# Splitting every third weight unit on GpSimd instead of VectorE: a two-layer hybrid decoder on one core

## The chip, the cores and the metric

The kernel runs on one core of a Trainium2 chip. The core has a matrix engine (TensorE, PE in the profile), three engines for elementwise work (VectorE or DVE, ScalarE or ACT, GpSimd or POOL), a queue that mostly issues DMAs (SyncE or SP), and 16 DMA engines. Every engine works through its own instructions in order, and waits on semaphores for the others. The metric is the device time of one execution in microseconds. The kernel before takes 1306.37 us, the median of three runs (1305.67 to 1306.95).

## What is computed

A trunk of two layers over 256 positions of width 2048, all in float32. Each layer adds a mixer's output to its scaled input and normalises the rows.

```python
for layer in range(DEPTH):                      # DEPTH = 2
    if layer % 2 == 0:
        h = ssd_moba_mixer(x, in0_w[i], ..., out0_w[i])
    else:
        h = s5_mixer(x, in1_w[i], ..., glu_w[i], out1_w[i])
    x = layer_norm(DEEPNORM_ALPHA * x + h, ln_g[layer], ln_b[layer])
```

The even layer projects x by one wide matrix (`in0_w`) to xs, z, B, C, dt and to queries, keys, values and a gate. xs, B and C pass a causal convolution and feed a state-space scan, whose result is gated by silu(z); the queries, keys and values feed attention; both results are mapped back by `out0_w`. The odd layer projects by `in1_w` to u and a gate, runs a diagonal complex scan, and then has three matrix products in a row: `y @ glu_w`, whose two halves make `ga * sigmoid(gb)` (the gated products), and, after a silu gate, `@ out1_w` (the last product).

## The kernel before

**Products in three parts.** TensorE is given its operands in the type fp32r. So that nearly all bits of float32 count, each operand is cut in two: a high part, the value copied to fp32r, and a low part, raw minus high. A product is then the sum of three: activations' high by weights' high, high by low, and low by high.

**Weight units.** The weights are read from memory in 462 units of 128 x 1024 elements (512 KB). They are numbered in the order in which TensorE uses them:

| units | what |
|---|---|
| 0 to 15 | B and C |
| 16 to 47 | xs |
| 48 to 79 | z |
| 80 to 207 | queries, keys, values, gates |
| 208 to 283 | out0 |
| 284 to 347 | in1 |
| 348 to 363 | first two blocks of the gated products |
| 364 to 429 | the other blocks of the gated products (66 units, `STREAM`) |
| 430 to 461 | out1, the last product |

**Making a unit ready.** `split_to(i)` traces, for each unit up to i, a load into a buffer `raw` (SyncE's queue, L361), the high part `wh` by ScalarE (L367), and the low part `wl` by VectorE (L372). For units 2 to 461 that is one instruction each, on 128 x 1024 elements. `raw`, `wh` and `wl` have four buffers each (`bufs=4`); each product calls `split_to(unit[0] + 3)`, so a unit is made ready about three units ahead of its use, and ScalarE can write `wh` of unit n only when TensorE is done with unit n - 4.

**Using a unit.** For xs and z (`product_wide`), a unit takes eight pairs of matmuls, one with `wh` (L478) and one with `wl` (L479). In the other products here a unit takes 12 matmuls (`xmm`, L422), a third of them with `wl`. In `STREAM` (`product_fast`), some steps work on sums of weight blocks and cover one half of the positions only: such a unit takes 6 matmuls (L521), two of them with `wl`, and is used up in half the time.

**Sums of weight blocks.** In the stream, the operand `raw` of a step is often a `block` that other blocks have been added to. Some of these sums are made by VectorE (L326), others by DMAs that add while they store. The adding DMAs are issued from GpSimd's queue (L324), each behind the split that still has to read the block, and in a fixed order among themselves.

**Order of the work.** The order of each engine's instructions is made when the program is built, by a scheduler that runs a model of the times; `tc.issue_after(ins)` keeps what is traced under it behind `ins` in the queue of `ins`'s engine, and is no wait for another engine. Elementwise work of the layers (`jobs`, `back`) is traced between the units by `run`, each piece behind the split instructions of the unit two ahead (`splits`).

**GpSimd's other work.** It computes part of softplus for dt (`soft2`, `soft3`, L734 to L745) while xs is being multiplied, adds up squares (L1092) in and after z, makes tables of phases (L906 to L909) and a rotary addition (L1143) during attention, and issues a part of the DMAs. It has no split.

The gated products are one stream of steps for three groups of two column blocks:

```python
HEAD = "p1 p1 n2 n2 p3 n2 p3 q5 q5 v2 v2 n2 q7 q7 p2 n1 n1 | p4 p4 p2 n1 n1".split()
FLOW = "q5 q5 p3 n2 p3 n2 v2 v2 n2 n2 q7 q7 p2 n1 n1 | p4 p4 p2 n1 n1".split()
```

Steps n1 and n2 are whole units, the others the half ones; "|" stands for the two p1 of the next group.

Of the kernel before, what the change touches and what calls it, by code (L numbers as in the profile page):

```python
# [9 lines left out]
F32 = mybir.dt.float32  # L10
F32R = mybir.dt.float32r
AF = mybir.ActivationFunctionType
OP = mybir.AluOpType
# [8 lines left out]
CU = KT // UK  # L22
# [15 lines left out]
def _stream():  # L38
    out, seen = [], {}
    for g in range(GROUPS):  # L40
        for s in FLOW if g else HEAD:
            names = [(g, s)] if s != "|" else [(g + 1, "p1")] * 2 * (g + 1 < GROUPS)
            for name in names:
                seen[name] = seen.get(name, -1) + 1
                out.append(name + (seen[name],))
    return out


STREAM = _stream()
# [140 lines left out]
def trunk(tc, io, out):  # L190
    nc = tc.nc
    V, A, G, T = nc.vector, nc.scalar, nc.gpsimd, nc.tensor
    count = [0]

    def nm(s):
        count[0] += 1
        return f"{s}_{count[0]}"

    with ExitStack() as top:
# [26 lines left out]
        units = []  # L226
# [7 lines left out]
        def hook(table, g, k, key, off, *what):  # L234
            table.setdefault(place[g, key, 0] + off, []).append((g, k, sources[g]) + what)
# [26 lines left out]
        chain = [len(units) + CU]  # L262
        units += [io["wglu"][i] for i in range(2 * CU)]
        start = len(units)
        place.update({key: start + i for i, key in enumerate(STREAM)})
        for g in range(GROUPS):
            n1, n2 = ([io["wglu"][CU * (2 + 2 * g + c) + u] for u in range(CU)] for c in range(2))
# [8 lines left out]
        for g in range(GROUPS):  # L276
            for k in range(2):
# [11 lines left out]
                hook(then, g, k, "p1", k, "add", "a", "b")  # L289
                hook(then, g, k, "v2", k, "add", "a", "d")  # L290
        units += [io["wo1"][i] for i in range(io["wo1"].shape[0])]
        ready = {}
        nsplit = [0]
        early = {}
        loaded = []
        conv = []
        splits = {}
# [7 lines left out]
        def prepare(*what):  # L305
            with ExitStack() as pin:
                if what[0] == 0:
                    pin.enter_context(tc.issue_after(tail["y"].ins))
                prepared(*what)
# [18 lines left out]
        def split_to(i):  # L328
            while nsplit[0] <= min(i, len(units) - 1):
                n = nsplit[0]  # L330
                for what in first.get(n, ()):
                    prepare(*what)
                if n in early:
                    with tc.issue_after(loaded[-1].ins):
                        early.pop(n)()
                if n in held_raw:
                    raw = blocks[held_raw[n]]
                elif n in room:
                    raw = keep[0].tile([P, UK, 512], F32R, tag=room[n], name=nm("raw")).bitcast(F32)
                else:  # L340
                    raw = st.tile([P, UK, 512], F32, tag="raw", name=nm("raw"))
                if n < 2:
                    wh = st.tile([P, UK, 512], F32R, tag="wh", name=nm("wh"))
                    wl = st.tile([P, UK, 512], F32R, tag="wl", name=nm("wl"))
                    for k in range(UK):
                        if k == 0:
                            xpart(n)
                        for lo, hi in ((0, 256), (256, 512)) if n + k == 0 else ((0, 512),):
                            loaded.append(nc.sync.dma_start(raw[:, k, lo:hi], units[n][:, k * 512 + lo : k * 512 + hi]))
                            with tc.issue_after(conv[-2].ins):  # L350
                                conv.append(A.activation(wh[:, k, lo:hi], raw[:, k, lo:hi], AF.Copy))
                            with tc.issue_after(conv[-2].ins):
                                conv.append(V.tensor_tensor(wl[:, k, lo:hi], raw[:, k, lo:hi], wh[:, k, lo:hi].bitcast(F32), op=OP.subtract))
                    ready[n] = (wh, wl)
                    nsplit[0] += 1
                    continue
                if n not in held_raw:
                    with ExitStack() as pin:
                        if n >= chain[0]:
                            pin.enter_context(tc.issue_after(loaded[-1].ins))  # L360
                        loaded.append(nc.sync.dma_start(raw.rearrange("p k n -> p (k n)"), units[n]))  # L361
                pool, th, tl = (keep[0], f"wh{n % 8}", f"wl{n % 8}") if n in keep[1] else (st, "wh", "wl")
                wh = pool.tile([P, UK, 512], F32R, tag=th, name=nm("wh"))
                with ExitStack() as pin:
                    if hold[1] is not None:
                        pin.enter_context(tc.issue_after(hold[1]))
                    high = A.activation(wh, raw, AF.Copy)  # L367
                wl = pool.tile([P, UK, 512], F32R, tag=tl, name=nm("wl"))
                with ExitStack() as pin:
                    if hold[0] is not None:  # L370
                        pin.enter_context(tc.issue_after(hold[0]))
                    splits[n] = (loaded[-1], high, V.tensor_tensor(wl, raw, wh.bitcast(F32), op=OP.subtract))  # L372
                ready[n] = (wh, wl)
                for what in then.get(n, ()):
                    prepare(*what)
                nsplit[0] += 1
# [72 lines left out]
        def product(kind, hl, nu=CU, prelude=None, first=WHOLE, due=None):  # L449
            ps = banks()  # L450
            for u in range(nu):
                if prelude:
                    prelude(u)
                split_to(unit[0] + 3)
                wpair = ready.pop(unit[0])
                if kind == "w":
                    wmm(ps, u, nu, hl, wpair, first if u == 0 else WHOLE)
                else:
                    last = u == nu - 1
                    steps = [(j, o) for o in range(2) for j in range(UK)] if last else [(j, o) for j in range(UK) for o in range(2)]  # L460
                    for j, o in steps:
                        xmm(ps, o, wpair, j, hl(u * UK + j), u == 0 and j == 0, last and j == UK - 1)
                unit[0] += 1
                pump((due - 1 if due and u < due - 1 else nu - 1) - u)
            return ps
# [186 lines left out]
        with ExitStack() as l0:  # L652
# [28 lines left out]
            def xpart(k):  # L681
                xr = a4([P, S])
                (nc.sync if k else nc.scalar).dma_start(xr, io["xt"][:, k, :])
                with ExitStack() as pin:
                    if k:
                        pin.enter_context(tc.issue_after(conv[-2].ins))
                    conv.append(A.activation(xh[:, k, :], xr, AF.Copy))
                with ExitStack() as pin:
                    if k:
                        pin.enter_context(tc.issue_after(conv[-2].ins))  # L690
                    conv.append(V.tensor_tensor(xl[:, k, :], xr, xh[:, k, :].bitcast(F32), op=OP.subtract))
# [339 lines left out]
            for j in range(4):  # L1031
                raw = sz[:, 4 * j : 4 * j + 4, :]
# [921 lines left out]
```

## Time and profile before

| | |
|---|---|
| median of three runs | 1306.37 us |
| span of the profiled execution | 1304.8 us |
| TensorE busy | 1296.0 us |
| VectorE busy | 1031.8 us |
| ScalarE busy | 738.1 us |
| GpSimd busy | 349.2 us |
| splits on VectorE (L372) | 460, mean 1.25 us |

The profile is of one execution; its times count from the first instruction. Busy times overlap, since the engines work side by side. A group's row gives, behind the count, its busy time and the mean of one instruction in nanoseconds, and then the idle time of the engine ahead of it with what ended it. In the timeline a row gives start, duration, engine, line, operation, output<-input, and in brackets the idle time before. TensorE's matmuls are pipelined and their ends are modelled, so that one may show 0.39 us where the next starts 0.23 us after it. The page can't be read as "TensorE has nothing to spare" from its busy share alone; who it waited for is a view of its own.

### The profile page before, as it was taken

The page shows a single profiled execution, that of the slowest core. Times are in us where ns is not written, and L with a number is a line of the kernel's source. Part 1 is how long each engine was busy: PE and PEld are TensorE (multiplying, and loading weights), DVE is VectorE, ACT ScalarE, POOL GpSimd, SP SyncE. Part 2 cuts the span into 40 slices and gives each one's busy share as a digit, 9 for nine tenths or more (in the row PEclk, how much of TensorE's full clock was granted, in tenths as well). Part 3 has the DMA queues.
Part 4 walks back from the last instruction along what each step waited for, and adds up shares of the span by engine and source line. Part 5 has one row for each costly group of instructions (what it writes and reads, how often), then busy time and mean ns, then how long its engine had stood idle before and what let it go on. Part 6 is the DMA issues. An engine that isn't in the chain of part 4 may idle for free.

```text
span 1304.8 us, 21605 instructions
## 1 busy us (share of the span) xinstructions
PE 1296.0 (99%) x7939; PEld 1089.7 (84%) x7939; DVE 1031.8 (79%) x1694; ACT 738.1 (57%) x1000; POOL 349.2 (27%) x649
## 2 busy tenths in 40 slices
PE   9999999999999999999999999999999999999997
PEld 9988888878888888888888888888888888888885
DVE  6778977885788888888877777858989859988665
ACT  6566668865644554464475555354355557666441
POOL 0044000125035767876820110022232001110000
PEclk9999999999999999999999999999999999999999
DMA  8555566565557766767768978469999789888762
GB/s 316 177 179 188 180 209 198 190 204 178 182 197 244 233 224 228 239 210 245 235 207 291 302 186 291 170 219 324 317 292 327 245 311 241 217 249 230 257 212 80
DMA packets 100094, 300.90 MB, mean 231 GB/s; under 512 B 19378, under 2 KB 29570, under 8 KB 99476
## 3 DMA queue, kind: packets, MB, share of 16 engines
q1 hardware_dynamic: 74356, 239.81, 55.0%
q0 software_dynamic: 11232, 46.18, 13.5%
q10 hardware_dynamic: 14400, 13.54, 3.2%
q8 instruction: 62, 1.02, 0.3%
q14 instruction: 44, 0.36, 0.1%
HBM read 276.93 MB, written 21.00 MB: 228 GB/s over the span
## 4 chain that ended last, share of the span: by engine, by line
PE 95%; POOL 2%; DVE 1%; DMA 1%; issue 0%; ACT 0%; SPq 0%; POOLq 0%
PE main L422 51%; PE main L478 17%; PE main L479 9%; PE main L521 7%; PE main L445 3%; PE aux L626 2%; POOL c L906 1%; PE aux L1084 1%; PE enc L1593 1%; PE dec L1638 1%; PE aux L982 1%; PE aux L1170 0%; DMA wb<-c 0%; POOL c L909 0%; DMA raw<-in_wi 0%; PE dec L1634 0%
## 5 line engine op out<-in xcount | busy, mean ns | idle before, releaser
L372 DVE TENSOR_TENSOR wl<-raw,wh 128x1024 fp32r<-128x1024 f32 x400 | 497.0, 1247 | 194.6 <-ACT wh L367 191.8
L367 ACT ACTIVATE wh<-raw 128x1024 fp32r<-128x1024 f32 x400 | 421.9, 1059 | 403.1 <-PE main L422 184.0
L422 PE MATMUL main<-wh,A 128*128 128x512 f32 x1216 | 392.5, 394 | 0.0
L478 PE MATMUL main<-A,wh 128*128 128x512 f32 x768 | 273.3, 400 | 0.0
L422 PEld LDWEIGHTS main<-wh,A 128*128 128x128 f32 x1216 | 227.9, 188 | 47.3 <-issue 0.7
L422 PE MATMUL main<-wh,C 128*128 128x512 f32 x832 | 265.1, 393 | 0.0
L422 PE MATMUL main<-wl,A 128*128 128x512 f32 x608 | 238.5, 392 | 0.0
L479 PE MATMUL main<-A,wl 128*128 128x256 f32 x768 | 215.5, 281 | 0.0
L422 PEld LDWEIGHTS main<-wh,C 128*128 128x128 f32 x832 | 155.9, 188 | 33.2
L478 PEld LDWEIGHTS main<-A,wh 128*128 128x128 f32 x768 | 144.2, 188 | 35.0 <-ACT b L1057 0.4
L422 PE MATMUL main<-wl,C 128*128 128x512 f32 x416 | 162.6, 391 | 0.0
L479 PEld LDWEIGHTS main<-A,wl 128*128 128x128 f32 x768 | 145.0, 189 | 0.4 <-issue 0.2
L422 PEld LDWEIGHTS main<-wl,A 128*128 128x128 f32 x608 | 114.3, 188 | 22.8 <-issue 0.2
L906 POOL TENSOR_TENSOR c<-c 128x8 f32<-128x8 f32 (+2 forms) x192 | 102.1, 550 | 27.8 <-DMA wb<-c 20.1
L422 PEld LDWEIGHTS main<-wl,C 128*128 128x128 f32 x416 | 78.1, 188 | 16.0
L372 DVE TENSOR_TENSOR wl<-block,wh 128x1024 fp32r<-128x1024 f32 x60 | 72.9, 1221 | 15.1 <-ACT wh L367 14.9
L367 ACT ACTIVATE wh<-block 128x1024 fp32r<-128x1024 f32 x60 | 63.1, 1060 | 36.5 <-PE main L422 20.1
L478 PE MATMUL main<-C,wh 128*128 128x512 f32 x192 | 68.3, 400 | 0.0
L1092 POOL TENSOR_TENSOR ssq<-ssq,c 128x256 f32<-128x256 f32 x16 | 18.0, 1128 | 161.1 <-ACT c L1090 160.4
L479 PE MATMUL main<-C,wl 128*128 128x256 f32 x192 | 53.5, 281 | 0.0
L908 POOL TENSOR_TENSOR c<-c,c 128x4 f32<-128x4 f32 (+2 forms) x96 | 42.2, 440 | 7.5
L324 POOL DMA_DIRECT2D block<-in_wglu x18 | 15.5, 916 | 104.0 <-DVE wl L372 86.7
(367 smaller groups left out, 1731.2 us busy)
## 6 DMA issues: line engine op xcount, KB each, us to landing
raw<-in_wi SPq DMA_DIRECT2D x270, 512.0 KB
raw<-in_wo SPq DMA_DIRECT2D x84, 512.0 KB
raw<-in_wglu SPq DMA_DIRECT2D x46, 512.0 KB
wt<-wb POOLq DMA_DIRECT2D x16, 896.0 KB, 8.3
block<-in_wglu POOLq DMA_DIRECT2D x20, 512.0 KB, 8.1
wb<-ob ACTq DMA_DIRECT2D x16, 512.0 KB
block<-in_wo POOLq DMA_DIRECT2D x12, 512.0 KB, 7.5
block<-in_wglu SPq DMA_DIRECT2D x12, 512.0 KB
```

The costliest lines, as they stand in the source:

```text
L324: added.append(nc.gpsimd.dma_start(blocks[g, name, k].rearrange("p k n -> p (k n)"), source[by][k], accum_op=OP.add))
L367: high = A.activation(wh, raw, AF.Copy)
L372: splits[n] = (loaded[-1], high, V.tensor_tensor(wl, raw, wh.bitcast(F32), op=OP.subtract))
L422: end = T.matmul(ps[o], l[:, k, sl], r[:, j, :], start=start and i == 0, stop=stop and i == 2, skip_group_check=free)
L445: T.matmul(pv[o // 2][:, o % 2, :], l[:, j, sl], r[:, k, :], start=first and i == 0 and o % 2 == 0, stop=end and i == 2 and o % 2 == 1, sk ...
L478: T.matmul(ps[o], wh[:, j, sl], xx[:, k, :, :].rearrange("p a n -> p (a n)"), start=first, stop=False, skip_group_check=True)
L479: lastmm[:] = [T.matmul(ps[o][:, S : 2 * S], wl[:, j, sl], xh[:, k, :], start=False, stop=end, skip_group_check=True)]
L521: lastmm[:] = [T.matmul(ps, p, q[:, j, :], start=begin, stop=False, skip_group_check=True)]
L626: end = T.transpose(dst[:, i * P : i * P + P], s, ident)
L906: G.tensor_tensor(p[:, :, :, 0:m], cs[:, :, :, 1 : m + 1], cs[:, i, :, n : n + 1].unsqueeze(1).to_broadcast([P, 2, 4, m]), op=OP.mult)
L908: G.tensor_tensor(cs[:, 0, :, n + 1 : n + 1 + m], p0[:, 0, :, 0:m], p1[:, 1, :, 0:m], op=OP.subtract)
L1092: G.tensor_tensor(ssq, ssq, jk[:, f, :], op=OP.add)
```

## The change

The low part of 44 of the 460 units is computed by GpSimd instead of VectorE: the same instruction, `wl = raw - wh`, on another engine's queue.

```diff
@@ -262,6 +262,7 @@
         start = len(units)
+        relief_from = start
         place.update({key: start + i for i, key in enumerate(STREAM)})
@@ -289,6 +290,7 @@
         units += [io["wo1"][i] for i in range(io["wo1"].shape[0])]
+        relief = set(range(24, 80, 3)) | set(range(len(units) - 2 * CU - 8, len(units) - 16, 3)) | set(range(relief_from + 2, start + len(STREAM), 3))
         ready = {}
@@ -369,7 +371,8 @@
                     if hold[0] is not None:
                         pin.enter_context(tc.issue_after(hold[0]))
-                    splits[n] = (loaded[-1], high, V.tensor_tensor(wl, raw, wh.bitcast(F32), op=OP.subtract))
+                    low = (G if n in relief else V).tensor_tensor(wl, raw, wh.bitcast(F32), op=OP.subtract)
+                    splits[n] = (loaded[-1], high, low)
                 ready[n] = (wh, wl)
```

With `len(units)` = 462, `start` = 364 and `CU` = 8 the set holds units 24, 27, ... 78 (19 units: eight of xs from 24 on, and eleven of z), 366, 369, ... 429 (22 units of the gated stream) and 438, 441 and 444 (three units of the second column block of the last product). No load, no high part and no matmul is changed. Since `run` queues a piece of elementwise work behind the split of a unit on that split's own engine, pieces traced behind one of the 44 are no longer tied to it on VectorE, and those on GpSimd are.

## The prediction

> **What bounds the kernel now.** I read the head of the page and its chain, then the waits of TensorE alone, then the timeline around the units that move.
>
> ```profile
> span 1304.8 us, 21605 instructions
> PE 1296.0 (99%) x7939; PEld 1089.7 (84%) x7939; DVE 1031.8 (79%) x1694; ACT 738.1 (57%) x1000; POOL 349.2 (27%) x649
> ...
> PE 95%; POOL 2%; DVE 1%; DMA 1%; issue 0%; ACT 0%; SPq 0%; POOLq 0%
> ...
> L372 DVE TENSOR_TENSOR wl<-raw,wh 128x1024 fp32r<-128x1024 f32 x400 | 497.0, 1247 | 194.6 <-ACT wh L367 191.8
> ```
>
> TensorE carries 95% of the chain that ended last. VectorE is 79% busy, but its largest group, the split (L372), sat 191.8 us waiting for the high parts. A busy PE could still hide stalls, so I asked who TensorE waited for:
>
> ```profile
> PE aux L626 <- POOL b L1143: 1.0, 1, 1.0
> ```
>
> No row of that view names a split on VectorE. The one wait that lies between the start and the end of the program is this one, for GpSimd, in the attention part, where nothing moves. So **the relief buys nothing**: every low part already comes in time. What can change the time is a low part that GpSimd delivers too late. The profiled execution spans 1304.8 us and the median is 1306.37, so 1.6 us are added at the end.
>
> **The change part by part.** 44 of 460 splits move: 19 in xs and z, 22 in the gated products, 3 in the last. VectorE loses 44 x 1.25 = 55 us. No row shows GpSimd doing a 1024-wide split, so I price it from its other two-operand instructions:
>
> ```profile
> 389.64 0.32 POOL L909 TENSOR_TENSOR c<-c,c 128x64 f32<-128x64 f32 x1
> 392.23 0.45 POOL L908 TENSOR_TENSOR c<-c,c 128x124 f32<-128x124 f32 x1
> 233.57 1.56 POOL L1092 TENSOR_TENSOR ssq<-ssq,c 128x256 f32<-128x256 f32 x2 [14.71 <-ACT c L1090]
> L1092 POOL TENSOR_TENSOR ssq<-ssq,c 128x256 f32<-128x256 f32 x16 | 18.0, 1128 | 161.1 <-ACT c L1090 160.4
> ```
>
> From 64 to 124 elements it is 0.13 / 60 = 2.2 ns each, so 0.45 + 900 x 0.0022 = **2.4 us**. The pair of 256 (0.78 each) gives 0.78 + 768 x 0.0024 = 2.6. The mean of L1092, 1.128 for 256, gives four times that, 4.5. I take 2.4 because that mean holds waiting, as the next rows show; 4.5 stays as the upper end, as no row here writes fp32r from GpSimd.
>
> ```profile
> 234.40 1.80 DVE L372 TENSOR_TENSOR wl<-raw,wh 128x1024 fp32r<-128x1024 f32 x1 [1.38 <-ACT wh L367]
> 245.99 1.22 DVE L372 TENSOR_TENSOR wl<-raw,wh 128x1024 fp32r<-128x1024 f32 x1 [1.17 <-ACT wh L367]
> 246.62 2.87 POOL L1092 TENSOR_TENSOR ssq<-ssq,c 128x256 f32<-128x256 f32 x2 [11.50 <-ACT c L1090]
> 247.46 1.44 DVE L372 TENSOR_TENSOR wl<-raw,wh 128x1024 fp32r<-128x1024 f32 x1 [0.25 <-ACT wh L367]
> ```
>
> A split that starts while GpSimd works takes 1.80 instead of 1.22, and GpSimd's pair takes 2.87 instead of 1.56 when splits run beside it. The two engines take turns at operands in SBUF. So a moved split can wait up to 1.2 us for its turn, and then holds back VectorE's next one by up to 2.4 us.
>
> *xs, z and the last product: hidden.* The unit with the least room there, but for the first, is 66 (the 65th split; its first use is the 401st matmul of L479; rows that begin with a stretch of time count one line's instructions up to there):
>
> ```profile
> 0.00:196.50 196.50, 78.99 (x64) 1.00 0.63 208
> 195.46 1.04 ACT L367 ACTIVATE wh<-raw 128x1024 fp32r<-128x1024 f32 x1
> 0.00:203.30 203.30, 112.03 (x400) 75.65 (x401) 1.00 0.63 208
> 203.41 0.28 PE L479 MATMUL main<-A,wl 128*128 128x256 f32 x1
> 1221.58 1.04 ACT L367 ACTIVATE wh<-raw 128x1024 fp32r<-128x1024 f32 x1
> 1228.83 0.39 PE L422 MATMUL main<-wl,C 128*128 128x512 f32 x1
> ```
>
> From the end of the high part (196.5) to the use are 6.9 us, and unit 438 of the last product (last two rows) has 6.2. A moved split needs 1.2 + 2.4 = 3.6, so 2.6 are left, also for a neighbour that it holds back. Its raw buffer comes free some 2 us later, so the load that SyncE queues for four units on, and the loads behind it, start later by that; the same lead covers them. Cost 0; with the 4.5 price still 0.
>
> *The first moved split, unit 24: not hidden.* GpSimd's first arithmetic instruction of the program is L734 now:
>
> ```profile
> 82.58 1.15 DVE L372 TENSOR_TENSOR wl<-raw,wh 128x1024 fp32r<-128x1024 f32 x1
> 82.79 8.14 POOL L734 TENSOR_TENSOR ew<-dw 32x256 f32<-32x256 f32 x1 [81.24 <-ACT a L780]
> 89.12 1.21 DVE L372 TENSOR_TENSOR wl<-raw,wh 128x1024 fp32r<-128x1024 f32 x1
> 91.00 0.67 POOL L735 TENSOR_TENSOR ew<-ew 32x256 f32<-32x256 f32 x1
> L734 POOLq MODIFY_POOL_CONFIG  x2: 11/11/11, 1.5 to 1.5; - x2
> ```
>
> It takes 8.14 us, where the same shape right after takes 0.67: **7.5 us more for being the first**. It did not hold the shared operands meanwhile, since VectorE's splits ran at 1.15 and 1.21. A setup instruction of GpSimd's queue (last row) stands before it alone. Now L734 needs its result only much later; its 7.5 us are hidden. After the change, unit 24's split is first. It is the 23rd split:
>
> ```profile
> 0.00:73.40 73.40, 26.91 (x22) 1.00 0.71 240
> 72.41 2.94 ACT L367 ACTIVATE wh<-raw 128x1024 fp32r<-128x1024 f32 x3
> 73.48 2.37 DVE L372 TENSOR_TENSOR wl<-raw,wh 128x1024 fp32r<-128x1024 f32 x2 [0.26 <-ACT wh L367]
> 0.00:78.40 78.40, 17.98 (x64) 12.23 (x65) 1.00 0.70 234
> 78.49 0.28 PE L479 MATMUL main<-A,wl 128*128 128x256 f32 x1
> ```
>
> It can start at 73.5, and TensorE wants it at 78.49 (the 65th matmul of L479). Ready at 73.5 + 7.5 + 2.4 = 83.4, it is **4.9 us late**, and TensorE, in order, stands still. Part of the 7.5 may be a turn lost to the last split before 90.3 (up to 1.2), so 3.7 to 4.9; I take 4.7. Unit 27 and the softplus chain queue behind it; TensorE's own delay covers the first and the long lead of the second the other.
>
> The Trainium skill, "GPSIMD Engine Reference", section 2.1, says that the first call of freshly loaded code adds about 6 us (5.95 measured) without a visible instruction. By that figure, an estimate, unit 24 would be 3.4 us late and the sum 1.3 lower; this case's trace shows the extra inside the instruction, as 7.5, and that is what I use.
>
> *The gated products: partly hidden.* Units are short here and the adding DMAs (L324) are issued by GpSimd itself, 0.85 us each. Tightest are units 375 (374th split; rows two to four), 405 (the next three; its high part is the first of the two) and 366 (the last two):
>
> ```profile
> 0.00:1098.60 1098.60, 463.74 (x373) 1.00 0.72 235
> 1097.40 1.05 ACT L367 ACTIVATE wh<-raw 128x1024 fp32r<-128x1024 f32 x1
> 1099.05 0.85 POOL L324 DMA_DIRECT2D block<-in_wglu  x1 [0.28 <-DVE wl L372]
> 1101.05 0.39 PE L422 MATMUL main<-wl,A 128*128 128x512 f32 x1
> 1154.12 2.00 ACT L367 ACTIVATE wh<-block 128x1024 fp32r<-128x1024 f32 x2
> 1154.98 0.86 POOL L324 DMA_DIRECT2D block<-in_wglu  x1 [0.87 <-DVE wl L372]
> 1157.54 0.39 PE L521 MATMUL main<-wl,A 128*128 128x512 f32 x1
> 1079.78 2.62 POOL L324 DMA_DIRECT2D block<-in_wglu  x3 [3.43 <-DVE wl L372]
> 1083.99 0.40 PE L422 MATMUL main<-wl,A 128*128 128x512 f32 x1
> ```
>
> If the DMA issue stays ahead of the split, 375 is ready at 1099.9 + 2.4 = 1102.3, 1.2 late (2.3 with a lost turn; 0 if it goes ahead of the DMA); 405 at 1155.84 + 2.4 = 1158.2, 0.7 late, with 0 to 1.1 for the neighbours it holds back; 366 at 1082.4 + 2.4 = 1084.8, 0.8 or 0. I take 1.2 + 1.0 + 0.4 and 0.4 for the other 19: **3.0**, with ends 0 and 6.
>
> The sum, on the profiled execution: 1304.8 + 4.7 + 3.0 = 1312.5; with the 1.6 outside it, **1314**.
>
> **The rivals.**
> *No first-call delay in timed runs* (the code is still there, or L734 was only kept waiting by VectorE's uninterrupted work from 82.6 to 90.3). Against it: GpSimd at 246.62 got its turn after one split. 1306.4 + 3.0 = 1309.4.
> *Not slower:* no first-call delay either, and the scheduler puts the splits of 366, 375 and 405 ahead of the DMA issues, or their rooms suffice. It decides at 2.6 us, the room of 375 from 1098.45 to 1101.05, against a price of 2.4. 1306.4. Speaking for it: with nothing ahead of it on GpSimd 375 would be in time, and 405 (room 2.4, from 1155.1) just so.
> *The turn-taking becomes the bound* in the gated products:
>
> ```profile
> 1080.00:1140.00 60.00, 60.00 (x274) 49.68 (x273) 54.35 (x61) 42.14 (x53) 9.26 (x11) 1.00 0.88 233
> 1140.00:1200.00 60.00, 60.00 (x271) 49.66 (x270) 50.65 (x55) 39.70 (x47) 5.16 (x6) 1.00 0.83 233
> ```
>
> VectorE is busy 54.4 and 50.7 of 60 us. Nine and thirteen moved splits, each 2.4 held for 1.2 freed, make 65 and 66 of 60 if all of VectorE's work waits. That is 11 us; work that reads PSUM doesn't wait, so about half: 1306.4 + 4.7 + 6 + some of the 3.0 = 1319.
> The Trainium skill, "SBUF — State Buffer", section "Who interferes with whom", speaks against the change here: a VectorE instruction with two SBUF inputs and a GpSimd instruction that reads SBUF exclude each other, and the second to come is blocked fully. The rows at 234.40 and 246.62 agree; held in full by all of VectorE's work it would make this rival 1306.4 + 4.7 + 11.5 = 1322.6.
> *GpSimd's split takes 4.5:* unit 24 is 6.8 late, and in the gated products the rooms, from 2.4 (405) and 2.6 (375) upward, fall short by up to 2.1; I put a mean of 0.7 on the 22 of them, 15 us, an estimate: 1328.
> *Faster:* only the 1.0 us wait of L626 could go, by a changed order; that is under the bound.
>
> **How the numbers follow.** Forecast (both delays) 0.48, the turn-taking bound 0.13, slow splits 0.10, no first-call delay 0.14, not slower 0.12, faster 0.03. A measurement of this kernel can tell about 0.2%, 2.6 us, from no change. Slower takes the first three and two thirds of the fourth: 0.80; same the rest of it and the fifth: 0.17; faster 0.03. The range runs from 1306.8, where only the last two and little of the fourth lie below, to 1326, which leaves out most of the slow splits: some 0.2 outside.
>
> **What would show it.** In the profile after: L372 on POOL 44 times near 2.4 us (waits included up to 3.6); the first one near 10 us, L734 near 0.7, and a TensorE wait of 4 to 5 us on POOL at 78 us; waits of about 1 us near units 366, 375 and 405; DVE's splits beside POOL's lengthened. Wrong, if TensorE waits for no POOL split, or waits in xs and z after unit 24.

## The result, and the profile after

The changed kernel takes **1323.78 us** (median of four runs, 1321.65 to 1323.88) beside 1306.66 us (median of four, 1305.67 to 1310.2) for the kernel before: a ratio of **1.0124, 95% interval 1.0106 to 1.0141**. It is 17.1 us slower by the medians. The forecast was 1314.0, so the direction and the range held, and the loss was more than twice what the terms of the sum came to.

The head of the page of the changed kernel, its chain and the larger group of the moved splits, 33 of the 44 (busy time, mean of one in ns, and GpSimd's idle time before them):

```profile
span 1322.1 us, 21636 instructions
PE 1300.9 (98%) x7939; PEld 1090.0 (82%) x7939; DVE 1052.1 (80%) x1650; ACT 735.2 (56%) x1000; POOL 459.3 (35%) x693
...
PE 69%; DVE 3%; issue 2%; POOL 1%; DMA 1%; ACT 0%; POOLq 0%; ACTq 0%; DVEq 0%
...
L374 POOL TENSOR_TENSOR wl<-raw,wh 128x1024 fp32r<-128x1024 f32 x33 | 88.7, 2687 | 197.5 <-ACT wh L369 195.6
```

(Behind the new line that sets `relief`, L293, line numbers are one to three higher than before: the split is L374, the high part L369.) The first thing to see is VectorE. It has 44 instructions fewer, and yet its busy time **rose**, from 1031.8 to 1052.1 us. At the 1.24 us that one of its 460 splits took before, the 44 should have taken 55 us off it, so 20.3 + 55 = 75 us were added to what it kept: 1.7 us for each moved split. The second is that TensorE fell from 95% to 69% of the chain. Whom it waited for:

```profile
PE aux L768 <- DVE dw L759: 3.7, 1, 3.7
PE main L524 <- DVE wl L374: 1.7, 2, 1.0
PE aux L1087 <- ACT b L1142: 1.6, 1, 1.6
PE turn L629 <- DVE sg L1803: 1.5, 1, 1.5
PE main L448 <- ACT wh L369: 1.5, 1, 1.5
PE aux L629 <- POOL b L1146: 1.3, 1, 1.3
PE main L524 <- DVE p L1845: 1.1, 1, 1.1
...
PE main L524 <- POOL wl L374: 0.7, 1, 0.7
```

The columns are total wait, count and longest. GpSimd's moved splits (the last row, and one more of 0.3) explain 1.0 us of it. Two rows left out (...) stand at the start and the end, in the kernel before as well, and the wait of L629 on GpSimd's `b` was 1.0 there. Most of the others name VectorE, on work that nobody moved.

Both kernels run the same 7939 matmuls, so the loss can be followed by the start of the n-th matmul (counted from 0) in the two traces, in us. The order is not quite the same: at 148 places another matmul stands, since the scheduler orders every engine's instructions anew for each kernel. This will matter below.

| matmul | before | after | behind by | what lies in between |
|---|---|---|---|---|
| 100 | 16.95 | 18.00 | 1.1 | TensorE waits for a high part at 12 us |
| 800 | 121.34 | 122.47 | 1.1 | xs; unit 24 is in here |
| 840 | 128.47 | 134.59 | 6.1 | the wait on the scan for dt (L768) |
| 1832 | 303.90 | 310.36 | 6.5 | z, queries, keys |
| 1840 | 304.82 | 313.04 | 8.2 | L1087 waits for ScalarE |
| 6990 | 1083.67 | 1092.40 | 8.7 | all up to the gated stream |
| 7600 | 1219.09 | 1236.87 | 17.8 | the gated stream |
| 7938 | 1298.78 | 1316.57 | 17.8 | the last product |

The first 1.1 us lies where the two programs do the same; it comes and goes between the kernels below (0 in two of the three others that were followed so) and is no part of the change. So there are two large places: **5.0 us at 122 to 134 us** and **9.1 us in the gated stream**, and a smaller one, 1.8 us at 304. At unit 24, where the forecast had 4.7 us, nothing is lost. Two windows of the gated stream after, to be laid beside the two that the prediction shows (equal times, not equal work: 258 and 248 matmuls here, 274 and 271 before):

```profile
1080.00:1140.00 60.00, 58.08 (x258) 46.72 (x256) 54.35 (x49) 39.30 (x50) 32.93 (x18) 1.00 0.83 226
1140.00:1200.00 60.00, 56.47 (x248) 45.04 (x249) 53.94 (x45) 38.51 (x48) 33.03 (x20) 1.00 0.83 219
```

The third pair is VectorE. Before, it was busy in the first window for 54.35 us with 61 instructions; now it is busy for the same 54.35 us with 49. Over equal work, matmuls 6990 to 7600, its busy time rose from 114.3 us (125 instructions) to 124.5 (103). The relief was eaten where it was given.

### The profile page after: what moved, and what is told of

The parts are those of the page before. It is cut to its first block, busy times and chain, and to the rows that moved or that the text cites. A ratio compares the mean times of both kernels' runs of the same rounds, so it can differ in the third digit from the quotient of the medians.

```text
span 1322.1 us, 21636 instructions
## 1 busy us (share of the span) xinstructions
PE 1300.9 (98%) x7939; PEld 1090.0 (82%) x7939; DVE 1052.1 (80%) x1650; ACT 735.2 (56%) x1000; POOL 459.3 (35%) x693
## 4 chain that ended last, share of the span: by engine, by line
PE 69%; DVE 3%; issue 2%; POOL 1%; DMA 1%; ACT 0%; POOLq 0%; ACTq 0%; DVEq 0%
PE main L425 46%; PE main L481 8%; PE main L524 5%; PE main L482 4%; PE aux L629 2%; DVE wl L374 2%; PE aux L985 1%; DMA block<-in_wglu 1%; PE enc L1596 1%; PE dec L1641 1%; PE aux L1205 1%; PE aux L1173 1%; POOL wl L374 0%; PE dec L1637 0%; ACT wh L369 0%
## 5 line engine op out<-in xcount | busy, mean ns | idle before, releaser
L369 ACT ACTIVATE wh<-raw 128x1024 fp32r<-128x1024 f32 x400 | 421.4, 1058 | 389.2 <-PE main L425 174.9
L374 DVE TENSOR_TENSOR wl<-raw,wh 128x1024 fp32r<-128x1024 f32 x367 | 482.4, 1320 | 186.7 <-ACT wh L369 184.4
L374 POOL TENSOR_TENSOR wl<-raw,wh 128x1024 fp32r<-128x1024 f32 x33 | 88.7, 2687 | 197.5 <-ACT wh L369 195.6
L425 PEld LDWEIGHTS main<-wl,A 128*128 128x128 f32 x608 | 114.3, 188 | 24.6 <-DVE wl L374 1.0
L909 POOL TENSOR_TENSOR c<-c 128x8 f32<-128x8 f32 (+2 forms) x192 | 99.2, 534 | 30.6 <-DMA wb<-c 22.9
L369 ACT ACTIVATE wh<-block 128x1024 fp32r<-128x1024 f32 x60 | 62.8, 1059 | 33.9 <-PE main L425 18.7
L374 DVE TENSOR_TENSOR wl<-block,wh 128x1024 fp32r<-128x1024 f32 x49 | 66.6, 1364 | 13.7 <-ACT wh L369 13.6
L911 POOL TENSOR_TENSOR c<-c,c 128x4 f32<-128x4 f32 (+2 forms) x96 | 46.6, 485 | 7.5
L326 POOL DMA_DIRECT2D block<-in_wo x12 | 10.4, 866 | 105.6 <-DMA raw<-in_wo 47.3
```

The costliest lines, as they stand in the source:

```text
L374: low = (G if n in relief else V).tensor_tensor(wl, raw, wh.bitcast(F32), op=OP.subtract)
L425: end = T.matmul(ps[o], l[:, k, sl], r[:, j, :], start=start and i == 0, stop=stop and i == 2, skip_group_check=free)
L909: G.tensor_tensor(p[:, :, :, 0:m], cs[:, :, :, 1 : m + 1], cs[:, i, :, n : n + 1].unsqueeze(1).to_broadcast([P, 2, 4, m]), op=OP.mult)
L911: G.tensor_tensor(cs[:, 0, :, n + 1 : n + 1 + m], p0[:, 0, :, 0:m], p1[:, 1, :, 0:m], op=OP.subtract)
```

## The experiments

Twelve kernels, all made from the changed one. Most have only another set of units in the line that sets `relief`; then the diff shows the new line alone. None was faster than the kernel before by more than can be told.

Times are given as the ratio to the kernel before, run beside it on the same chip, and as us of 1306.

| kernel | ratio, 95% interval | us |
|---|---|---|
| xs and z alone (19 units) | 1.0055 (1.0039 to 1.0072) | +7.2 |
| z and the last product alone (14) | 1.0007 (0.9998 to 1.0016) | +0.9 |
| unit 24 alone | 0.9999 (0.9990 to 1.0009) | -0.1 |
| units 30, 33, 36, 39 alone | 1.0015 (1.0006 to 1.0025) | +2.0 |
| xs and z without these four | 1.0027 (1.0016 to 1.0038) | +3.5 |
| gated products alone (22) | 1.0063 (1.0048 to 1.0078) | +8.2 |
| the 12 roomy ones of them | 1.0015 (1.0006 to 1.0024) | +2.0 |
| the 10 tight ones of them | 1.0038 (1.0024 to 1.0053) | +5.0 |
| the 22 in two halves each | 1.0052 (1.0034 to 1.0070) | +6.8 |
| no split moved, GpSimd subtracts beside | 1.0126 (1.0111 to 1.0141) | +16.5 |
| no split moved, GpSimd fills memory beside | 1.0001 (0.9991 to 1.0010) | +0.1 |
| no split moved, GpSimd's first instruction early | 1.0008 (0.9998 to 1.0019) | +1.0 |

The theory after the comparison of the traces was that GpSimd and VectorE keep each other from operands in SBUF for whole instructions, so that a moved split takes from VectorE more than it gives. Its rivals were the two of the forecast (a delay of GpSimd's first instruction; moved splits late by their own length) and that GpSimd's queue, which also issues the adding DMAs, is held up. A fourth has to be kept in view: that the scheduler's new order of the other engines costs time. No kernel was built for it, but the traces show in which kernels the order changed.

### Is there a delay of the first instruction?

Unit 24 alone:

```diff
+        relief = {24}
```

> Unit 24 alone. Theory of the first instruction: unit 24's split takes about 10 us, TensorE waits 4 to 5 us at 78 us, the first softplus instruction of GpSimd then takes 0.7; +4.7 us. Theory now (the 8.14 us before were GpSimd kept out by VectorE's unbroken work): the split takes 2.4 us at 74, the first softplus instruction behind it still takes several us if VectorE's splits stand back to back beside it, about 0.7 to 1.6 if the order there has gaps; the time within 1.5 us of before.

No change in time. The split took 2.40 us at 73.84, and the first softplus instruction (L737, L734 before) 1.94 instead of 8.14. That alone spoke for neither, since L737 wasn't first any more. So the kernel before was given a small product ahead of it:

```diff
+        relief = set()
...
             G.memset(ones, 1.0)
+            G.tensor_tensor(ones, ones, ones, op=OP.mult)
```

> The kernel before (no split on GpSimd) with one small GpSimd product of 128 x 128 right after its memsets at 1.5 us, so that the first softplus instruction is no longer GpSimd's first. If the 8.14 us were the price of being first: the small product takes some 6 us or more and the softplus instruction under 2. If they were GpSimd kept out by VectorE's unbroken row of work from 82.58 to 90.25: the small product takes under 1 us and the softplus instruction still 8.1, as long as VectorE's row there is the same. The time: no change.

The timeline of GpSimd, then that of VectorE, in this kernel (start, duration, line, operation, output<-input):

```profile
1.63 0.40 POOL L1043 TENSOR_TENSOR ones<-ones 128x128 f32<-128x128 f32 x1
83.03 8.13 POOL L737 TENSOR_TENSOR ew<-dw 32x256 f32<-32x256 f32 x1 [81.00 <-ACT a L783]
91.24 0.67 POOL L738 TENSOR_TENSOR ew<-ew 32x256 f32<-32x256 f32 x1
```

```profile
82.82 1.15 DVE L374 TENSOR_TENSOR wl<-raw,wh 128x1024 fp32r<-128x1024 f32 x1
83.89 3.21 DVE L786 SCALAR_TENSOR_TENSOR a<-D,params,a 128x255 f32<-128x255 f32 x8
87.04 1.21 DVE L374 TENSOR_TENSOR wl<-raw,wh 128x1024 fp32r<-128x1024 f32 x1
88.17 1.25 DVE L786 SCALAR_TENSOR_TENSOR a<-D,params,a 128x253 f32<-128x253 f32 x3
89.35 1.20 DVE L374 TENSOR_TENSOR wl<-raw,wh 128x1024 fp32r<-128x1024 f32 x1
90.49 0.40 DVE L493 TENSOR_TENSOR D<-D,main 128x256 f32<-128x256 f32 x1
```

GpSimd's first product took 0.40, and L737 still 8.13; the time is the same within its interval. Read the second fence for the reason. From 82.82 to 90.49 VectorE runs 14 instructions that take two tensors from SBUF, and each starts a little before the last one ends (82.82 + 1.15 = 83.97, and the next starts at 83.89). The first that has one of its inputs in PSUM is L493 at 90.49. GpSimd ends at 83.03 + 8.13 = 91.16, which is 90.49 + 0.67, the time that L738 takes without any wait. So L737 **waited 7.46 us for VectorE** and then worked for 0.67. The kernel before fits in the same way: VectorE's first instruction with an input in PSUM starts there at 90.25, and 90.25 + 0.67 = 90.92 is where the 8.14 us end (82.79 + 8.14 = 90.93).

The kernel with units 30 to 39 alone shows it from the other side. There L737 is GpSimd's first product again, and VectorE's order has a break one instruction behind its split:

```profile
82.84 1.93 POOL L737 TENSOR_TENSOR ew<-dw 32x256 f32<-32x256 f32 x1 [81.29 <-ACT a L783]
```

```profile
82.63 1.15 DVE L374 TENSOR_TENSOR wl<-raw,wh 128x1024 fp32r<-128x1024 f32 x1
83.71 0.46 DVE L786 SCALAR_TENSOR_TENSOR a<-D,params,a 128x255 f32<-128x255 f32 x1
84.88 0.27 DVE L758 MEMSET dw<- 32x256 f32 x1 [0.71 <-POOL ew L737]
```

First, and done in 1.93. The delay belongs to VectorE's unbroken row of work, not to being first. One thing stays open: with unit 24 alone VectorE's row was unbroken too, and GpSimd got in after the first L786. What decides at such a seam, these runs don't show.

### xs and z

```diff
+        relief = set(range(24, 80, 3))
```

> The 19 units of xs and z alone (24, 27, ... 78). Theory as predicted (delay of the first GpSimd instruction, everything else there hidden): +4.7 us, in one TensorE wait at 78 us. Theory now (GpSimd and VectorE take turns at SBUF, and three moved splits fall into the softplus chain): a TensorE wait of 3 to 4 us at 122 to 126 us, some 1 to 2 us at 312, no wait at 78; +6 to +8 us. Rival (the 17 us of the whole change come from the gated products alone): within 1.5 us of before.

```diff
+        relief = set(range(48, 80, 3)) | set(range(len(units) - 2 * CU - 8, len(units) - 16, 3))
```

> The 11 units of z and the three of the last product alone. As predicted: no cost (room of 6.2 us and more against 3.6). Theory now: the same, within 1.5 us of before, since VectorE has gaps there; the first GpSimd split at 153 us takes 2.4 to 3 us. Rival (each moved split costs something wherever it stands, 17 / 44 = 0.4 us): +5.5 us.

The first gave +7.2 us with a wait of 3.6 us on the scan (L759) and none at 78; the second nothing that can be told from no change. So z and the last product, moved by themselves, are hidden, as predicted; it takes the eight units of xs to bring the loss. Then the four whose splits stand in GpSimd's softplus chain, alone and left out:

```diff
+        relief = {30, 33, 36, 39}
```

> Units 30, 33, 36 and 39 alone. If these make the chain for dt late: the wait of 3 to 4 us at 122 to 126 us and the lower clock behind it, +4 to +6 us with no other unit moved. Rival: under +1.5 us.

```diff
+        relief = set(range(24, 80, 3)) - {30, 33, 36, 39}
```

> xs and z without units 30, 33, 36 and 39, whose splits stood between the softplus instructions on GpSimd. If these four make the chain for dt late: no TensorE wait on the scan at 122 to 126 us, no lower clock behind it, +0 to +2 us. Rival (VectorE is held back by all of the xs splits): the wait stays at 2 us or more, +4 us or more.

Alone, they make TensorE wait for the scan by 1.1 us and cost 2.0, less than expected. Without them that wait is gone, but 3.5 us remain, more than expected. The wait of 3.6 needs both, the four and the rest. Nor is it the four splits' length alone that brings it, as the kernel before will show. The timeline of the changed kernel shows the last links, GpSimd first:

```profile
103.67 2.38 POOL L374 TENSOR_TENSOR wl<-raw,wh 128x1024 fp32r<-128x1024 f32 x1
...
112.41 0.72 POOL L748 TENSOR_TENSOR ew<-ew 32x256 f32<-32x256 f32 x1
113.10 2.39 POOL L374 TENSOR_TENSOR wl<-raw,wh 128x1024 fp32r<-128x1024 f32 x1
```

```profile
113.17 2.60 DVE L754 SCALAR_TENSOR_TENSOR ew<-ew,dw 32x256 f32<-32x256 f32 x1 [2.37 <-POOL ew L748]
115.70 2.83 DVE L786 SCALAR_TENSOR_TENSOR a<-D,params,a 128x254 f32<-128x254 f32 x7
...
124.37 1.01 DVE L757 TENSOR_SCALAR dw<-ew,ea 32x256 f32<-32x256 f32 x1 [2.04 <-ACT ea L756]
125.31 0.40 DVE L493 TENSOR_TENSOR D<-D,main 128x256 f32<-128x256 f32 x1
125.64 0.67 DVE L759 TENSOR_TENSOR_SCAN dw<-dw 32x256 f32<-32x256 f32 x1
```

A moved split is between the softplus steps at 103.67. VectorE stands still for 2.37 us until the chain is through at 113.13. Its next step, 32 x 256 like the rest, then takes 2.60 us because GpSimd has just started the next moved split (113.10 + 2.39 = 115.49). The seven convolution steps queued behind it, ScalarE's silu behind those, and ScalarE's `ea` behind the silu are late in turn, and the scan comes at 125.64, where TensorE has been waiting since 122.7.

The kernel before shows that this is not only a chain made late. GpSimd's last step, VectorE's step behind it, the scan, and TensorE's first use of the scan were there:

```profile
111.15 0.73 POOL L745 TENSOR_TENSOR ew<-ew 32x256 f32<-32x256 f32 x1
118.55 0.40 DVE L751 SCALAR_TENSOR_TENSOR ew<-ew,dw 32x256 f32<-32x256 f32 x1
119.75 0.68 DVE L756 TENSOR_TENSOR_SCAN dw<-dw 32x256 f32<-32x256 f32 x1
123.56 0.24 PE L765 MATMUL aux<-consts,dw 32*128 32x32 f32 x1
```

GpSimd was through at 111.88, only 1.3 us earlier than after the change, and 1.1 of these are the loss at the start. But VectorE came to its step 6.7 us later than that, since nine more convolution steps stood ahead of it, and TensorE asked for the scan 3.1 us after its end, with matmul 811. In the changed kernel the scheduler has put VectorE's step ahead of those nine, so that VectorE stands still for GpSimd, and TensorE's matmul at place 801, ten places earlier, which were 2.0 us of work before. **Both shifts are in the three kernels that wait here** (the changed one, xs and z, the four units) and in none of the other ten or in the kernel before. So 2.0 of the 3.7 us are TensorE asking earlier; with the four units alone, where GpSimd was through at 109.52, they are more than the whole 1.1. The other 1.7 are left of a scan that ends 4.8 us later (the 1.1 taken off), against the 3.1 that it had in hand. How much of the 4.8 comes from VectorE's new order and how much from instructions held back beside GpSimd, such as the 2.60, no run separates.

What is left without the four units is shown in that kernel, in z at 178 us (GpSimd, then VectorE):

```profile
177.89 2.40 POOL L374 TENSOR_TENSOR wl<-raw,wh 128x1024 fp32r<-128x1024 f32 x1 [3.38 <-ACT wh L369]
```

```profile
177.57 0.27 DVE L886 TENSOR_TENSOR a<-lap 128x64 f32<-128x64 f32 x1
177.76 0.26 DVE L887 TENSOR_TENSOR a<-lap 128x64 f32<-128x64 f32 x1
178.06 2.35 DVE L888 TENSOR_TENSOR lap<-a,a 128x64 f32<-128x64 f32 x1
180.29 1.21 DVE L374 TENSOR_TENSOR wl<-raw,wh 128x1024 fp32r<-128x1024 f32 x1
```

An instruction of 64 elements goes from 0.27 to 2.35 us because GpSimd was there first, and the split behind it makes TensorE wait 1.3 us. The same happens with all of xs and z moved (2.40 us, and a wait of 1.3 at 188), but not with z and the last product, so a moved split in z isn't free wherever it falls. The profiled execution of this kernel took 1307.48 against a median of 1308.88, so where the rest of the 3.5 lies isn't shown.

### The gated products: late low parts, or VectorE held back?

```diff
+        relief = set(range(relief_from + 2, start + len(STREAM), 3))
```

> The 22 units of the gated products alone (366, 369, ... 429). As predicted (a few units late by their own longer split): +3.0 us, all TensorE waits on GpSimd's splits. Theory now (each of GpSimd's 2.4 us keeps VectorE out, and VectorE has few gaps there): +8 to +11 us, most of it in waits on VectorE's splits or its other work. Rival (the displacement that xs and z leave behind costs in the stream too): clearly under 8 us.

+8.2 us, and with the 7.2 of xs and z this makes 15.4 of the 16.2 that the ratio of the whole change gives, so the two places add up. Here too the order changed, on TensorE at 120 places. The wait on `sg` (1.4 us in this kernel), for one, comes from both: VectorE's step for it took 2.88 us instead of 0.68, and TensorE asks five matmuls earlier, 1.1 us of work before. To part lateness from holding back, the 22 were divided by the room that they had before, from the end of the high part to the use, 4.5 us being the line (unit 414 with 4.25 us and unit 390 with 4.58 fell on the wrong side of it):

```diff
+        relief = {369, 381, 387, 393, 396, 399, 411, 414, 417, 420, 426, 429}
```

> In the gated products only the 12 units whose high part lay 4.5 us and more ahead of the use in the profile of before (369, 381, 387, 393, 396, 399, 411, 414, 417, 420, 426, 429). If the cost is the moved split's own lateness: 0 to +1 us, since 2.4 us fit in 4.5. If it is VectorE held back by GpSimd's turns: about 12/22 of the 8.2 us of all 22, +4 to +5 us, in waits on VectorE.

```diff
+        relief = {366, 372, 375, 378, 384, 390, 402, 405, 408, 423}
```

> The other 10 units of the gated products alone (366, 372, 375, 378, 384, 390, 402, 405, 408, 423), whose high part lay under 4.5 us ahead of the use; with the 12 roomy ones they make the 22. If every GpSimd read there costs the same: 10/22 of 8.2 us, +3.7 us. If the price falls where the room is short: what the roomy ones (+2.0) leave of 8.2, +6 us. If the tight ones are merely late by themselves, as predicted: +3.0 us, in waits on GpSimd's splits.

The roomy ones cost 2.0 and the tight ones 5.0. Neither theory had the first right: it is more than lateness allows, and less than an equal share. But the waits name VectorE in both (1.9 us on one split of its own with the roomy ones; 1.6 on its splits against 0.5 on GpSimd's with the tight ones). Both kernels have a changed order too, so the shares are not exact prices. How that looks, in the kernel with all 22, GpSimd, VectorE and TensorE around unit 407:

```profile
1165.89 2.89 POOL L374 TENSOR_TENSOR wl<-raw,wh 128x1024 fp32r<-128x1024 f32 x1 [0.24 <-issue]
```

```profile
1165.30 1.21 DVE L374 TENSOR_TENSOR wl<-block,wh 128x1024 fp32r<-128x1024 f32 x1
1166.44 3.42 DVE L374 TENSOR_TENSOR wl<-raw,wh 128x1024 fp32r<-128x1024 f32 x1
```

```profile
1168.53 0.39 PE L524 MATMUL main<-wh,A 128*128 128x512 f32 x1
1169.91 0.50 PE L524 MATMUL main<-wl,A 128*128 128x512 f32 x1 [1.00 <-DVE wl L374]
```

GpSimd makes unit 408, which TensorE uses only at 1171.63, 2.85 us after it is done. Nobody waits for it. But VectorE's split of unit 407 takes 3.42 instead of 1.2, and TensorE waits for that one. To measure the holding back by itself, no split was moved, and for the same 22 units GpSimd read beside VectorE for nobody:

```diff
-                    low = (G if n in relief else V).tensor_tensor(wl, raw, wh.bitcast(F32), op=OP.subtract)
+                    low = V.tensor_tensor(wl, raw, wh.bitcast(F32), op=OP.subtract)
                     splits[n] = (loaded[-1], high, low)
+                if n in relief:
+                    idle = gpool[-1].tile([P, 512], mybir.dt.bfloat16, tag="idle", bufs=1, name=nm("idle"))
+                    for k in range(UK):
+                        G.tensor_tensor(idle, wh[:, k].bitcast(F32), wh[:, k].bitcast(F32), op=OP.subtract)
```

> All splits stay on VectorE; for the 22 units of the gated products GpSimd makes two subtractions of 128 x 512 from the high part into a tile that nobody reads (some 2.6 us per unit), when that high part is there. If lateness of the moved low parts is the cost: within 1.5 us of before, since nobody waits for these results. If GpSimd's turns hold VectorE back: more than the 8.2 us of the moved splits, since VectorE keeps its own 22 as well; +9 to +30 us, the waits on VectorE's splits.

**+16.5 us, although no low part is moved.** It is twice what the 22 moved splits cost, and here VectorE keeps its own 22 as well; the waits are on VectorE's splits (6.2 us in eight waits). The order can't be the cause here: TensorE, VectorE and ScalarE run the same instructions in the order of the kernel before, as far as the traces name them, and so they do in the control that comes next. The control keeps GpSimd as busy, and its queue as full, but with memory writes (the subtraction cut to 128 x 8, so that it still starts on the high part):

```diff
+                    G.tensor_tensor(idle[:, 0:8], wh[:, 0, 0:8].bitcast(F32), wh[:, 0, 0:8].bitcast(F32), op=OP.subtract)
+                    for k in range(5):
+                        G.memset(idle, 0.0)
```

> As the kernel in which GpSimd works beside the gated products for nobody, but what it does for each of the 22 units is a subtraction of 128 x 8 from the high part and then five memsets of 128 x 512, about 2.6 us that read nothing. If GpSimd's operand reads hold VectorE back: 0 to +3 us. If it is GpSimd's queue being held up (its adding DMAs are issued later): +10 to +16 us, as with the subtractions.

+0.1 us. The groups of GpSimd's dummy work in the stream (1085 to 1230 us), first with subtractions, then with memory writes:

```profile
L379 POOL TENSOR_TENSOR idle<-wh 128x512 bf16<-128x512 f32 x43 | 69.5, 1617 | 36.3 <-ACT wh L369 34.6
```

```profile
L380 POOL MEMSET idle<- 128x512 bf16 x107 | 59.5, 556 | 5.7
L378 POOL TENSOR_TENSOR idle<-wh 128x8 bf16<-128x8 f32 x21 | 20.4, 971 | 21.5 <-ACT wh L369 20.9
```

GpSimd was busier in the second (59.5 + 20.4 = 79.9 us against 69.5), so a full queue is not the cause. VectorE's splits on blocks (1080 to 1230 us) in the kernel before, with subtractions, and with memory writes:

```profile
L372 DVE TENSOR_TENSOR wl<-block,wh 128x1024 fp32r<-128x1024 f32 x34 | 41.2, 1221 | 2.7 <-ACT wh L367 2.5
```

```profile
L374 DVE TENSOR_TENSOR wl<-block,wh 128x1024 fp32r<-128x1024 f32 x35 | 52.5, 1512 | 0.1
```

```profile
L374 DVE TENSOR_TENSOR wl<-block,wh 128x1024 fp32r<-128x1024 f32 x34 | 41.0, 1219 | 3.7 <-ACT wh L369 3.5
```

Reading lengthens them from 1221 to 1512 ns, writing leaves them at 1219. It is GpSimd's **reading of SBUF** that costs. The Trainium skill, "SBUF — State Buffer", section "Who interferes with whom", says just this: a VectorE instruction with two SBUF inputs contends with a GpSimd instruction that reads SBUF, not with one that only writes. These three rows agree.

Last, whether shorter instructions on GpSimd would let VectorE through:

```diff
+                    if n in relief:
+                        for k in range(UK):
+                            low = G.tensor_tensor(wl[:, k], raw[:, k], wh[:, k].bitcast(F32), op=OP.subtract)
+                    else:
+                        low = V.tensor_tensor(wl, raw, wh.bitcast(F32), op=OP.subtract)
```

> The 22 units of the gated products, each low part on GpSimd in two instructions of 128 x 512. If VectorE is held back by one GpSimd instruction at a time: VectorE's longest splits fall from 3.7 to about 2.5 us and the time to +4 to +6 us. If the price is the total of GpSimd's reading: +8 us as with whole ones, or +9 with the second fixed cost.

+6.8 us (4.4 to 9.1) beside +8.2 (6.3 to 10.2) with whole ones: no difference that can be told. VectorE's longest split was 4.31 us, not 2.5: it starts at 1176.58, GpSimd's two halves run in one row from 1176.97 to 1179.80, and the split ends at 1180.89, about one undisturbed split later. So halving did not let VectorE in between; that the price goes by the total of what GpSimd reads fits this, but a finer cut was not tried.

## Why the prediction was right or wrong, point by point

- **The bound** (TensorE, so the relief can buy nothing): right, and stronger than put. There was no relief; VectorE's busy time rose by 20 us.
- **The price of a split on GpSimd, 2.4 us** from the slope of the small products: right. The first one took 2.40 with unit 24 alone; the mean of 2.69 for the 33 holds waiting.
- **"The first moved split, unit 24: not hidden", 7.5 us "for being the first"**: this step failed. Nothing was lost there. What the forecast took for a start-up delay was GpSimd kept out by VectorE. Its argument, that VectorE's splits ran at 1.15 and 1.21 meanwhile and so GpSimd held nothing, was read the wrong way round: VectorE ran at full speed because it never let go. The rival "no first-call delay" had named the unbroken work from 82.6 to 90.3 as the other reading. The 6 us for a first call that the prediction cited from the Trainium skill, "GPSIMD Engine Reference", section 2.1, show in no run here: the first product took 0.40.
- **xs and z otherwise hidden, "the long lead" covers the softplus chain**: failed for xs, and with it the term "Cost 0". In place of the 4.7 us at 78 us stand 5.0 at 122 to 134 us, at the scan for dt. The lead was there (6.7 us on VectorE, 3.1 on TensorE), but in the order of the kernel before; the forecast took that order as fixed, and the scheduler's new one gave away all of VectorE's lead and 2.0 us of TensorE's. It also counted the room of the units alone, and not that of VectorE's other work, which the moved splits hold back. The sign that the prediction had named for being wrong, a wait in xs and z after unit 24, is this one. That nothing was lost at 78 us and something of the same size at 122 is chance. z and the last product by themselves: right (+0.9, not told from zero).
- **The gated products, 3.0 us**: the term was mis-sized, 8.2 measured. It summed the lateness of moved splits, and TensorE waited for those by 1.0 us in all. Most of the rest are waits on VectorE's work, held back beside them, and a part, such as 1.1 us before `sg`, is TensorE asking earlier in the changed order; the 8.2 us are not divided between the two. But that reading beside VectorE can by itself cost this much is shown, with the order unchanged (16.5 us). The forecast had priced the holding back as a rival ("the turn-taking becomes the bound", 6 us for the half of it that reads SBUF, 11 to 11.5 in full) and gave it 0.13. The rows at 234.40 and 246.62 that it quotes for turns already told against its 0.4 us for 19 units.
- **The sum**: 4.7 + 3.0 forecast, 7.2 + 8.2 measured by the parts alone.
- The 1.8 us at matmul 1840 (L1087 waiting for ScalarE) were not forecast. TensorE waits there for ScalarE's second rotary step (L1142), and ScalarE's work around it runs 2.3 us late, from a step on that waits for a DMA (at 304.00, 295.26 before, with 6.5 us of the difference lost earlier). What made that late is not shown.

## What to carry to other kernels

Before work is moved from VectorE to GpSimd, look at where its operands lie: with inputs in SBUF on both sides the two engines shut each other out for whole instructions, and here 1.25 us of relief cost VectorE 1.7 us of waiting. Count the room not only of the moved instruction, but of everything that VectorE has queued in the 2.4 us beside it, down to a 64-element step on a long chain. A lone instruction that takes ten times its usual time is to be held against the other engine's timeline before it is called a start-up cost. And where a scheduler makes the order, a change of one queue can move work in all of them: compare the orders before a wait is put down to the instruction that was moved.

## What the runs showed of the hardware that was not expected

GpSimd can lose its turn many times in a row: 14 VectorE instructions and 7.46 us, until one came that reads PSUM.

A stand-still of TensorE can cost more than its length. The windows behind the wait on the scan, in the changed kernel, and in the one with four units, where the wait was 1.1 us (third column from the end: granted clock):

```profile
127.00:132.00 5.00, 5.00 (x21) 4.33 (x20) 3.39 (x9) 1.44 (x4) 0.36 (x1) 0.66 0.84 267
```

```profile
127.00:132.00 5.00, 5.00 (x30) 4.34 (x29) 4.23 (x9) 3.60 (x9) 0.00 (x0) 1.00 0.55 206
```

After 3.7 us without work the granted clock was 0.66 in the next window, and 21 matmuls ran where 30 run otherwise. It added 1.3 us to the 3.7 (from 4.79 behind at matmul 801 to 6.12 at 840).
